# Odd layer attention: the rest of the queries on both partition halves, second score product over 128 rows

## The chip, the cores and the metric

The kernel runs on one core of one Trainium2 chip, as one program for the whole computation. The metric is the device time of one execution in microseconds (us), taken as the median of the runs shown; less is better. TensorE (PE in the profile) does the matrix products and the transposes, VectorE (DVE) and ScalarE (ACT) read its results out of PSUM, GpSimd (POOL) works on SBUF only, and SyncE (SP) issues the DMAs. Each engine works off its own queue in the order in which the program put it there.

## What is computed

Two blocks of layers on 512 tokens of width 1024. The first block has four layers, the second has an even and an odd one, each followed by a feed-forward part. The change lies in the mixer of the odd layer, which has eight heads of neighbourhood attention and eight heads of grouped-query attention, each with 64 features. Cut to what matters:

```python
def odd_mixer(u_lat, u_ctx, need_ctx, w_in, w_out, rpb, q_norm, k_norm, rope):
    lat = split_cols(u_lat @ w_in, ODD_SPLITS)
    ctx = split_cols(u_ctx @ w_in, ODD_SPLITS)
    c_lat = neighbourhood_attention(q, k, v, k_ctx, v_ctx, rpb)      # 8 heads: bias, 512 keys + 256 context keys
    d_lat = blocked_attention(qd_l, concat(kd_c, kd_l), concat(vd_c, vd_l), GQA_DIM ** -0.5)   # 8 heads, 2 key heads
    return concat(c_lat, d_lat) @ w_out

# per head, for 128 queries at a time
s = (q @ k.T) * scale (+ bias)      # 768 keys: 512 tokens and 256 of the context
p = softmax(s)
o = p @ v
```

## The kernel before

Products are taken in the type float32r. To keep the precision of float32, an operand x is held as two parts, the leading part h (x rounded to float32r) and the rest l = x - h, and a product is the sum of the products of the parts.

The odd layer has the stages `oddkv` (keys and values), `oddq` (queries), `odda` (attention), `out` (output projection) and then `ffn`. In `odda` (`odd_attn`, `odd_pair`, `attend`) the 16 heads are taken in 8 pairs, pairs 0 to 3 neighbourhood heads, pairs 4 to 7 grouped-query heads. The two heads e = 0, 1 of a pair lie on partitions 0 to 63 and 64 to 127. Each pair goes through 4 query tiles of 128 queries. For a query tile and a head, `attend` has two score products, one of 512 and one of 256 keys, each in a PSUM bank of its own; then `softmax` (DVE takes the maximum, line 852, or with the bias added, line 1071; then the negated maximum, line 857; ACT the exponential with its sum, line 864; DVE the reciprocal, lines 869 and 871); then `turned` (TensorE transposes the result, line 889; DVE copies 256 columns out, line 891, ACT 512, line 893); then the product with the values (line 1080). At the end of a pair, line 878 spreads the reciprocals over the partitions, line 1085 copies them and line 1086 multiplies. Four PSUM banks (`pp`) serve the scores, four (`pa`) all else.

The operands of a pair are made by `odd_operands` one pair ahead. `attn_keys` gives, for head e, one tile with the leading part of its keys on the head's own half of the partitions and the rest of its keys on the other half (lines 1871, 1872, both on DVE). `attn_queries` gives, for head e, a tile `hi[e]` with the leading part of its queries on both halves (line 1856 on DVE, line 1857 on ACT), and one tile `lo` for both heads, the rest of head e's queries on its own half (line 1858 on POOL). So one product over 128 rows, line 1881, yields qh·kh + qh·kl, and a second one over the head's own 64 rows, line 1882, adds ql·kh. Both add up in the same PSUM bank:

```python
nc.tensor.matmul(ps, qh[e][:, s], kap, start=True, stop=False)      # 128 rows, line 1881
nc.tensor.matmul(ps, ql[r, s], kap[r], start=False, stop=True)      # 64 rows, line 1882
```

The operand tiles are taken from the pools that also hold weights, by tag, with `NBUF` buffers each: `cwr` 3, `cwh` 2, `cwl` 2, `wh` 4, `wl` 4. Pairs with an even number use the tags with a c, odd ones the others (the keys of the grouped-query heads are made once for two pairs). A new tile of a tag waits until the tile whose buffer it takes has been read for the last time. The order of the instructions on each engine is laid down when the program is built, by a planner that puts them in the order of its own estimate of the times.

Of the kernel before, what the change touches and what calls it, by code (L numbers as in the profile page):

```python
# [22 lines left out]
SEQ = 512  # L23
# [12 lines left out]
class Split:  # L36
    """An operand held as two float32r parts, [128, k, n] in pieces along k."""
# [11 lines left out]
class Residual:  # L49
    """The residual stream: in SBUF between a layer's end and the next norm, else in DRAM."""  # L50
# [13 lines left out]
    def store(self, t, dst=None):  # L64
        """Token tile t goes to DRAM (a new version at t = 0)."""
        if t == 0:
            n = self.core.nm("res_" + self.key)
            self.new = dst if dst is not None else self.core.dp.tile([self.nt * 128, D], F32, name=n, tag=n)
        n = 1 if dst is None else 2
        for i in range(n):  # L70
            cs = slice(i * D // n, (i + 1) * D // n)
            self.core.nc.sync.dma_start(self.new[t * 128:(t + 1) * 128, cs], self(t)[:, cs])
        if t == self.nt - 1:
            self.src = self.new


class Core:
# [21 lines left out]
    def phase(self, name, gen):  # L99
        """gen, its tiles named after it."""  # L100
# [21 lines left out]
    def bank(self, use, shape, dt):  # L122
        """A PSUM bank of the groups that the use has, by turns."""
# [15 lines left out]
    def setup(self):  # L139
        """What the first norm waits for: its condition, its modulation, x."""  # L140
# [27 lines left out]
        for v in (1, 0):  # L168
# [5 lines left out]
            # column 2g + h of the vector lies in row 32g of half h  # L174
# [10 lines left out]
    def setup2(self):  # L185
# [9 lines left out]
        # a norm's root is taken of the sum of squares, not of their mean  # L195
# [6 lines left out]
    def condition(self, name, srcs):  # L202
        """silu of condition columns, padded to 32 columns so that a column group is whole."""
# [12 lines left out]
    def columns(self, key, parts):  # L216
        """Vectors of 128-blocks -> columns over partitions, one transpose for all."""
# [17 lines left out]
    def rstd1(self, ss, n, eps=EPS):  # L235
        """(ss / n + eps) ** -0.5 for a [128, 1] column."""
# [7 lines left out]
    def rstdN(self, ss, n, width, c=1.0, eps=EPS):  # L244
        """c * (ss / n + eps) ** -0.5 for [128, width]."""
# [13 lines left out]
    def lo_engine(self, ph):  # L259
        """The engine of the next subtraction, by turns."""  # L260
        ph = self.sk + ph
        pat = LO.get(ph, LO.get(self.sk, LO[""]))
        i = self.nlo[ph] = self.nlo.get(ph, -1) + 1
        return self.nc.gpsimd if pat[i % len(pat)] == "p" else self.nc.vector

    def weights(self, W, k0, nk, c0, n, held=False):
        """Rows k0*128.. of W, columns c0.., as split parts [128, nk, n]."""
# [7 lines left out]
    def wsplit(self, src, nk, n, held=False):  # L275
        """src [128, a, b] in DRAM, a * b = nk * n -> split parts [128, nk, n]. Held ones leave the next ones room."""
# [11 lines left out]
    def proj_tok(self, H, nt, W, K, c0, n, out, r0=0, each=None, inturn=False, lead=1):  # L288
        """out[0] = PSUM tiles [128, 2, n], two token tiles each, by columns c0..c0+n (rows r0*128.. of W).
        With each, out[0] is by token tiles and each(t) is called for every one; in turn, one is finished  # L290
        before the next starts."""
# [32 lines left out]
        for i in range(0, len(ks), lead):  # L324
            ws = [(k0, nk, self.weights(W, r0 + k0, nk, c0, n)) for k0, nk in ks[i:i + lead]]
            for t in range(nt):
                # a PSUM bank holds two token tiles as one accumulation group
# [7 lines left out]
    def proj_T(self, H, ntok, W, K, cols, out, m=128):  # L335
        """out[0] = PSUM [m, ntok] each, columns cols[i].. of W on partitions."""
# [5 lines left out]
    def cols_T(self, o, H, W, K, c0, m):  # L342
        """o = columns c0..c0+m of H @ W, transposed."""
# [12 lines left out]
    def halves_T(self, o, H, Ws, K, n):  # L356
        """cols_T of the first 128 columns of several matrices, one half of the tokens before the other."""
# [15 lines left out]
    def mods(self, scr, cname, W, ncond, v):  # L373
        """Vector v of cond @ W into DRAM scr [ncond, .. * 1024] (bias not yet added)."""
# [20 lines left out]
    # Background work: queues of generators, of which step takes a step now and then.  # L395
# [20 lines left out]
    def drain(self, gen):  # L416
        """Runs gen, background work after each of its steps."""
# [7 lines left out]
    def mod_cols(self, scr, ic, b, v0, pre):  # L425
        """Columns A = pre * (1 + scale), B = shift; shift at vector v0, scale at v0 + 1."""
# [13 lines left out]
    def gate_row(self, scr, ic, b, v, post):  # L440
        """32 * gate * post over all partitions, [128, 1024]."""
# [21 lines left out]
    def prenorm(self, x, nt, m):  # L463
        """x(t) [128, 1024] per token tile -> H, a Split of the modulated norm, transposed.
        Returns (H, step), step(t) for each token tile once x(t) is there."""
# [17 lines left out]
        def turn(xs, s):  # L483
            """Token tiles xs, normed, into H."""
# [26 lines left out]
    def normed(self, x):  # L511
        """x / its root of the sum of squares."""
# [14 lines left out]
    def rstd2(self, a, b):  # L527
        """(a + b) ** -0.5 for columns."""
# [6 lines left out]
    def outproj(self, O, nt, W, K, x, gg, nxt=None, dst=None):  # L535
        """x(t) += rms(O @ W) * gg; nxt() gives the norm that follows, fed tile by tile. Returns its H."""
# [30 lines left out]
    def first(self, n):  # L567
        """What is put out now comes before the last n instructions."""
        return self.tc.high_priority(offset=n) if n else nullcontext()

    def partial(self, ssp, nt):
        """The first three parts of the sums of squares, and what keeps the root from zero."""
# [6 lines left out]
    def postnorm(self, yg, a, b, x):  # L579
        """x += (a + b) ** -0.5 * yg."""  # L580
# [6 lines left out]
    def silu2(self, dst, z):  # L587
        """dst = 2 * silu(z), z may sit in PSUM."""
# [4 lines left out]
    def newO(self, nt=4):  # L593
        """A mixer's output, transposed, in pieces that come into being with their first write."""
# [3 lines left out]
    def Opiece(self, O, k, nt=4):  # L598
        """Where rows k * 128.. of the output go."""
# [12 lines left out]
    def Odone(self, O, p, nt=4):  # L612
        """Piece p is complete: split."""
# [7 lines left out]
    def gla(self, H, j, O):  # L621
# [13 lines left out]
        for h in range(4):  # L635
            v = []
            if h == 0:
                # a projection by token tiles is the first to start
# [21 lines left out]
    def gla_decay(self, H, j, b):  # L660
        """b: per head the logarithm of the decay, summed up in chunks of 128, times 16."""
        nc, A = self.nc, self.A
        W = A["gla_w_in"][j]
        # low-rank decay
# [31 lines left out]
    def gla_pairs(self, b, qT, kT, out):  # L696
# [9 lines left out]
        for lv in range(7):  # L706
# [14 lines left out]
            for c in range(4):  # L721
                # the later tokens of a pair of blocks against the earlier ones
# [120 lines left out]
    def softmax(self, heads, scale, rl, first=None):  # L843
        """heads: (P, parts) each, P [128, ..] taking exp(scale * (s - max)) of the parts in turn;
        rl [128, heads] takes 1 / sum. first: per head a [128, 2] whose column 0 is the first part's maximum."""
# [27 lines left out]
    def rows(self, rl):  # L873
        """Columns rl [128, query tile, 2] of two heads as rows over the heads' partitions, in PSUM."""
# [7 lines left out]
    def turned(self, pt, P, n):  # L882
        """pt [128, n] = P', by 128 columns."""
# [12 lines left out]
    def fox_forget(self, H):  # L896
        """-8 times the summed logarithms of the forget gates, [head, token] in DRAM."""
# [22 lines left out]
    def fox(self, H, O):  # L920
        nc, A = self.nc, self.A
        W = A["fox_w_in"][0]
        # the gains of queries and keys, over two heads
# [7 lines left out]
        for g in range(4):  # L931
# [16 lines left out]
            # a projection that needs no norm follows each that does  # L948
# [24 lines left out]
    def fox_queries(self, x, gain):  # L973
        """A head pair's queries x [128, token tile, 128] as parts, transposed, [.., head, token]: h and l; h and
        two ones. The gain is that of queries and keys."""
# [11 lines left out]
    def fox_decays(self, F):  # L987
        """A tile for fox_keys' second result, with the parts of the heads' F."""
# [8 lines left out]
    def fox_keys(self, x, KB):  # L997
        """Keys, likewise: h and h; l and the parts of the heads' F."""
# [10 lines left out]
    def fox_pair(self, hp, ops, v, zg, out):  # L1009
        """Attention of heads 2hp and 2hp + 1 of a group; zg: twice their gates, transposed."""  # L1010
# [4 lines left out]
        for it in range(4):  # L1015
# [4 lines left out]
            for e in range(2):  # L1020
                ps = (self.psP if FOXS else self.psA)()
                # at least 256 columns, where float32r takes a cycle each
# [19 lines left out]
    def transposes(self, src, nt):  # L1042
        """src(t) [128, m] per token tile -> PSUM [m, nt * 128]."""
# [7 lines left out]
    def attend(self, out, nq, scores, keys, v, nj, scale, bias=None):  # L1051
        """scores(e, it, ps, keys): query tile it's products; keys(e) -> [(AP, n)], one PSUM bank each; v(e, j) [128, 64].
        out [128, nq * 128]: the heads' outputs on partition halves."""
# [35 lines left out]
    def rope(self, x, n, cs):  # L1089
        """In place on x [128, t, h, 2n], cs = (cos, sin) [128, t, n]."""  # L1090
# [11 lines left out]
    def gsplit(self, hi, lo, src, g):  # L1102
        """Split src * g, g per partition."""
# [63 lines left out]
    def gdn_proj(self, H, nt, key, st):  # L1167
        """Projections, convolution, normalisation: q, k, v by tokens, decays by rows and columns."""
# [28 lines left out]
        # suffix sums for the backward rows: total - prefix + own  # L1197
# [23 lines left out]
        # what the later stages of a head pair or group take waits in DRAM for its turn  # L1221
# [23 lines left out]
    def gdn_cols(self, H, st, cols):  # L1245
        """q, k or v (0, 1, 2) of head pairs: [(which, pair)]. A projection's convolution runs under the next
        one's products, and only then it is turned."""
# [25 lines left out]
    def gdn_put(self, st, sv, cols):  # L1273
        """Column blocks by tokens, normalised, to DRAM."""
# [31 lines left out]
    # The delta rule runs in chunks, both directions, on groups of nh heads (nh * nt = 8). A unit u of  # L1306
    # a group is a head and a token tile; with a half e of the tile's partitions it is a chunk of 64
    # tokens. Direction d = 1 runs from the last token to the first.
# [4 lines left out]
    def gdn_decay(self, st, g):  # L1313
        """exp(-|gc_p - gc_f|) between the tokens of a group's chunks."""
# [21 lines left out]
    def gdn_front(self, st, g, E):  # L1336
        """Decayed products k k' and k q' of a group's chunks, the former cut in 32 x 32 blocks."""
# [43 lines left out]
    def gdn_subst(self, st, s):  # L1381
        """(I + M)^-1 of the 32 x 32 diagonal blocks of two groups, one block a partition, by forward
        substitution; a backward block is taken transposed. M[c, s] = beta_c Gd[c, s];
        R = (I + M)^-1 diag(beta)."""
# [38 lines left out]
    def gdn_steps(self, st, g, out):  # L1423
        """The inverse's blocks put together, the step matrices."""
# [855 lines left out]
```

## Time and profile before

| | us |
|---|---|
| median of 3 runs | 3319.11 |
| lowest and highest of the 3 | 3316.0, 3320.16 |
| span of the profiled execution, first to last instruction | 3315.4 |
| PE busy in the span | 3154.1 (95%) |
| PE weight load busy | 2704.3 (82%) |
| DVE busy | 1699.2 (51%) |
| ACT busy | 1451.7 (44%) |
| POOL busy | 1307.3 (39%) |

The profiled execution's span is 3315.4 us; what its time holds beside the span is not shown by itself. In the profile, a line such as `L1882` is a line of the kernel, `odda.pp` a tile of stage `odda`, `64*128` the rows and columns of the array that a product takes, and the figures behind it partitions x elements of what is streamed. The matmul records overlap, since their ends are modelled: the time that a product takes from the next one is read from the starts, or from the chain, whose pieces follow each other without overlap. The chain (or critical chain) is the work that ended last, followed back: each piece is what the next one waited for.

### The profile page before, as it was taken

The numbers are of one execution on the slowest core, as the hardware profiler recorded it, in microseconds if no ns is written. First come the engines' busy times: TensorE is split into PE (matmuls) and PEld (weight loads), VectorE is DVE, ScalarE is ACT, GpSimd is POOL, SyncE is SP. The second block draws the span as 40 slices with busy tenths as digits, with TensorE's granted clock in tenths as the row PEclk, the third lists the DMA queues.
The fourth block names the chain that finished last, engine by engine and source line by source line (L and its number), as shares of the span: only waits on it lengthen the run. The fifth ranks groups of instructions, "written<-read, shape, count | busy, mean of one in ns | idle before, by whom it ended". The sixth has DMA issues, their size and how long they took to land.

```text
span 3315.4 us, 63038 instructions
## 1 busy us (share of the span) xinstructions
PE 3154.1 (95%) x24399; PEld 2704.3 (82%) x24399; DVE 1699.2 (51%) x3578; ACT 1451.7 (44%) x3189; POOL 1307.3 (39%) x1320
## 2 busy tenths in 40 slices
PE   7999999899999999988989999899999989999999
PEld 4878889778778778887877899889889956789898
DVE  3744564454555555657888667531215476541112
ACT  3434544455444533345545544543325246543323
POOL 2544453322222344443642123554446510154445
PEclk9999999999999999998999999899999979999999
DMA  7355645754436524444753344433333310043332
GB/s 239 87 159 185 194 144 164 234 173 125 147 111 198 162 81 132 153 117 126 188 172 110 86 131 114 155 115 94 117 101 124 102 39 1 25 142 94 98 119 89
DMA packets 487155, 426.36 MB, mean 129 GB/s; under 512 B 108038, under 2 KB 441065, under 8 KB 486857
## 3 DMA queue, kind: packets, MB, share of 16 engines
q1 hardware_dynamic: 486857, 422.35, 42.5%
q8 instruction: 192, 3.15, 0.4%
q14 instruction: 106, 0.87, 0.1%
HBM read 383.66 MB, written 38.03 MB: 127 GB/s over the span
## 4 chain that ended last, share of the span: by engine, by line
PE 75%; DVE 11%; DMA 5%; ACT 4%; issue 3%; POOL 2%; SPq 1%; POOLq 0%; DVEq 0%; ACTq 0%
PE ffn.pp L352 6%; PE ffn.pp L351 6%; PE ffn.pp L353 5%; PE ffn.pp L308 3%; PE ffn.pp L307 3%; PE ffn.pp L309 3%; PE mods.pa L386 3%; PE out.pp L307 2%; PE out.pp L309 2%; PE out.pp L308 2%; DMA mods.wm<-in_w_mod_dram 2%; PE odda.pa L889 1%; PE fox.pp L308 1%; PE fox.pp L309 1%; PE fox.pp L307 1%
## 5 line engine op out<-in xcount | busy, mean ns | idle before, releaser
L257 POOL TENSOR_TENSOR ffn.wl<-ffn.wr,ffn.wh 128x512 fp32r<-128x512 f32 x258 | 333.5, 1294 | 355.0 <-ACT ffn.wh L256 355.0
L256 ACT ACTIVATE ffn.wh<-ffn.wr 128x512 fp32r<-128x512 f32 x258 | 162.5, 631 | 354.9 <-PE ffn.pp L353 144.3
L351 PE MATMUL ffn.pp<-pre.t,ffn.wh 128*128 128x512 f32 x672 | 261.5, 389 | 0.0
L352 PE MATMUL ffn.pp<-pre.t,ffn.wl 128*128 128x512 f32 x672 | 261.5, 389 | 0.0
L353 PE MATMUL ffn.pp<-pre.t,ffn.wh 128*128 128x512 f32 x672 | 261.4, 389 | 0.0
L308 PE MATMUL ffn.pp<-ffn.wl,ffn.t 128*128 128x256 f32 x656 | 185.3, 283 | 0.0
L309 PE MATMUL ffn.pp<-ffn.wh,ffn.t 128*128 128x256 f32 x656 | 184.9, 283 | 0.0
L307 PE MATMUL ffn.pp<-ffn.wh,ffn.t 128*128 128x256 f32 x656 | 184.7, 283 | 0.0
L591 DVE SCALAR_TENSOR_TENSOR ffn.t<-ffn.t,ffn.pp 128x512 f32<-128x512 f32 (+1 forms) x66 | 39.4, 596 | 252.2 <-ACT ffn.t L590 252.1
L257 POOL TENSOR_TENSOR gla.wl<-gla.wr,gla.wh 128x512 fp32r<-128x512 f32 x66 | 87.2, 1321 | 163.7 <-ACT gla.wh L256 158.5
L307 PE MATMUL gla.pp<-gla.wh,pre.t 128*128 128x256 f32 x512 | 149.4, 292 | 0.7 <-ACT gla.t L644 0.4
L308 PE MATMUL gla.pp<-gla.wl,pre.t 128*128 128x256 f32 x512 | 148.8, 291 | 0.0
L309 PE MATMUL gla.pp<-gla.wh,pre.t 128*128 128x256 f32 x512 | 148.4, 291 | 0.0
L353 PEld LDWEIGHTS ffn.pp<-pre.t,ffn.wh 128*128 128x128 f32 x672 | 126.2, 188 | 26.2
L351 PEld LDWEIGHTS ffn.pp<-pre.t,ffn.wh 128*128 128x128 f32 x672 | 126.2, 188 | 26.1
L352 PEld LDWEIGHTS ffn.pp<-pre.t,ffn.wl 128*128 128x128 f32 x672 | 126.2, 188 | 25.8
L257 POOL TENSOR_TENSOR ffn.cwl<-ffn.cwr,ffn.cwh 128x512 fp32r<-128x512 f32 x44 | 60.3, 1370 | 212.4 <-ACT ffn.cwh L256 183.9
L386 PE MATMUL mods.pa<-mods.wm,cond_c 128*32 128x256 f32 x1408 | 121.4, 398 | 16.8 <-DMA mods.wm<-in_w_mod_dram 16.7
L1133 DVE SCALAR_TENSOR_TENSOR ffn.t<-ffn.t,ffn.pp 128x512 f32<-128x512 f32 (+1 forms) x66 | 39.4, 597 | 176.3 <-PE ffn.pp L353 175.7
L256 ACT ACTIVATE ffn.cwh<-ffn.cwr 128x512 fp32r<-128x512 f32 x132 | 82.9, 632 | 102.8 <-PE ffn.pp L353 43.0
L308 PEld LDWEIGHTS ffn.pp<-ffn.wl,ffn.t 128*128 128x128 f32 x656 | 125.9, 192 | 0.2
L307 PEld LDWEIGHTS ffn.pp<-ffn.wh,ffn.t 128*128 128x128 f32 x656 | 125.6, 192 | 0.2
(786 smaller groups left out, 10843.8 us busy)
## 6 DMA issues: line engine op xcount, KB each, us to landing
mods.wm<-in_w_mod_dram SPq DMA_DIRECT2D x176, 512.0 KB
gla.wr<-in_gla_w_in_dram SPq DMA_DIRECT2D x96, 256.0 KB
ffn.wr<-in_w_ffn_gate_dram SPq DMA_DIRECT2D x88, 256.0 KB
ffn.wr<-in_w_ffn_up_dram SPq DMA_DIRECT2D x88, 256.0 KB
ffn.wr<-in_w_ffn_down_dram SPq DMA_DIRECT2D x88, 256.0 KB
fox.wr<-in_fox_w_in_dram SPq DMA_DIRECT2D x64, 256.0 KB
sgu.wr<-in_sgu_w_in_dram SPq DMA_DIRECT2D x48, 256.0 KB
out.res_x<-out.t SPq DMA_DIRECT2D x24, 512.0 KB
```

What stands on the lines that cost most here:

```text
L256: nc.scalar.activation(hi, src, AF.Copy)
L257: (lo_eng or nc.vector).tensor_tensor(lo, src, hi.bitcast(F32), op=ALU.subtract)
L307: nc.tensor.matmul(o, H.hi(kk, s), w[0][:, k], start=(kk == 0 and first), stop=False)
L308: nc.tensor.matmul(o, H.hi(kk, s), w[1][:, k], start=False, stop=False)
L309: nc.tensor.matmul(o, H.lo(kk, s), w[0][:, k], start=False, stop=(kk == K - 1 and last))
L351: nc.tensor.matmul(o, wh[:, k], H.hi(kk), start=(kk == 0), stop=False)
L352: nc.tensor.matmul(o, wl[:, k], H.hi(kk), start=False, stop=False)
L353: nc.tensor.matmul(o, wh[:, k], H.lo(kk), start=False, stop=(kk == K - 1))
L386: nc.tensor.matmul(ps[g * 32:(g + 1) * 32, :256], pad[:, j, :], ws[j][:, g * 256:(g + 1) * 256], start=(j == 0), stop=(j == 7))
L591: nc.vector.scalar_tensor_tensor(dst, dst, 1.0, z, ALU.add, ALU.mult)
L889: nc.tensor.transpose(pz[:, j:j + 128], P[:, j0 + j:j0 + j + 128], self.ident)
L1133: nc.vector.scalar_tensor_tensor(f, sg, 0.5, o[1], ALU.mult, ALU.mult)
```

## The change

`attn_queries` holds the rest of the queries in one tile for each head. The subtraction of line 1858 writes it on the head's own half as before, and a new instruction on ACT copies it to the other half. Line 1882 then takes all 128 rows of that tile and of the keys, and so adds ql·kh + ql·kl. The tags of the rests are `cwr` and `cwh` in even pairs (before, `cwh`), `wh` and `wl` in odd ones (before, `wh`). The diff also takes out comments and docstrings all over the file and leaves the line numbers up to this place; of code it has only this:

```diff
@@ def attn_queries(self, q, par):
         hi = [self.w(("cwr", "wh")[par], 1, n)[:, 0] for _ in range(2)]
-        lo = self.w(("cwh", "wh")[par], 1, n)[:, 0]
+        lo = [self.w(tag, 1, n)[:, 0] for tag in (("cwr", "cwh"), ("wh", "wl"))[par]]
         for e in range(2):
             r, z = self.H4(e), self.H4(1 - e)
             nc.vector.tensor_copy(hi[e][r], q[r])
             nc.scalar.copy(hi[e][z], q[r])
-            nc.gpsimd.tensor_tensor(lo[r], q[r], hi[e][r].bitcast(F32), op=ALU.subtract)
+            nc.gpsimd.tensor_tensor(lo[e][r], q[r], hi[e][r].bitcast(F32), op=ALU.subtract)
+            nc.scalar.copy(lo[e][z], lo[e][r].bitcast(F32))
         return hi, lo
@@ def odd_pair(self, hp, st, O, q, keys):
         def scores(e, it, ps, kap):
-            s, r = slice(it * 128, (it + 1) * 128), self.H4(e)
+            s = slice(it * 128, (it + 1) * 128)
+
             nc.tensor.matmul(ps, qh[e][:, s], kap, start=True, stop=False)
-            nc.tensor.matmul(ps, ql[r, s], kap[r], start=False, stop=True)
+            nc.tensor.matmul(ps, ql[e][:, s], kap, start=False, stop=True)
```

## Rows read from the trace of the kernel before

**Rows 1.** The page: the span, and the shares of the whole chain by engine

```profile
span 3315.4 us, 63038 instructions
...
PE 75%; DVE 11%; DMA 5%; ACT 4%; issue 3%; POOL 2%; SPq 1%; POOLq 0%; DVEq 0%; ACTq 0%
```

**Rows 2.** Stretches: length, busy us of PE, PEld, DVE, ACT, POOL, clock, DMA

```profile
2663.40:2683.40 20.00, 20.00 (x71) 12.37 (x72) 10.54 (x37) 7.11 (x21) 0.00 (x0) 0.58 0.10 30
...
2700.80:2719.90 19.10, 19.10 (x87) 12.67 (x88) 9.86 (x36) 9.28 (x27) 0.00 (x0) 0.65 0.00 0
2719.90:2727.40 7.50, 7.32 (x57) 5.08 (x57) 7.15 (x19) 3.93 (x10) 2.66 (x2) 1.00 0.01 2
...
2801.80:2824.60 22.80, 22.65 (x165) 15.41 (x165) 13.58 (x46) 14.16 (x40) 0.88 (x1) 1.00 0.01 2
...
2663.40:2882.20 218.80, 212.35 (x1512) 145.33 (x1513) 144.03 (x466) 126.81 (x344) 25.56 (x17) 0.93 0.03 9
```

**Rows 3.** The chain between 2700 and 2880 us, shares by line

```profile
by line: PE odda.pa L889 23.4%; PE odda.pa L1080 18.6%; PE odda.pp L1882 18.5%; PE odda.pp L1881 12.5%; DVE odda.mx L852 3.7%; issue 3.5%; PE odda.pa L878 2.8%; ACT odda.at L864 2.3%; DVE odda.at L891 2.2%; DVE odda.wh L1871 1.7%; DVE odda.
```

**Rows 4.** The chain in order of time, pair 5: start us, us, what

```profile
2815.19 0.59 PE odda.pa L889 x4
2815.77 0.23 PE odda.pp L1881
2816.00 0.42 PE odda.pp L1882
2816.42 0.37 PE odda.pa L889 x2
2816.79 0.12 PE odda.pp L1881
2816.91 0.31 PE odda.pp L1882
...
2818.46 0.31 PE odda.pp L1881
...
2821.50 0.58 PE odda.pa L1080 x6
2822.09 0.43 PE odda.pp L1882
```

**Rows 5.** Source line 1882, one of its forms: duration ns least/median/most, starts, form

```profile
L1882 PE MATMUL odda.pp<-odda.wl,odda.wh x24: 490/497/792, 2689.2 to 2875.4; 64*128 64x512 f32 x24
```

**Rows 6.** Source line 1025, the second score product of stage fox

```profile
L1025 PE MATMUL fox.pp<-fox.t,fox.t x64: 278/342/628, 728.3 to 1011.7; 66*128 66x256 f32 x32, 66*128 66x384 f32 x16, 66*128 66x512 f32 x16
```

**Rows 7.** The chain at the end of stage fox, first products of out

```profile
1011.63 0.23 PE fox.pp L1024
1011.86 0.23 PE fox.pp L1025
...
1013.35 0.12 PE out.pp L308
```

**Rows 8.** Timeline of DVE in pair 5

```profile
2818.50 0.69 DVE L852 TENSOR_REDUCE odda.mx<-odda.pp 128x1 f32<-128x512 f32 x1 [0.62 <-PE odda.pp L1882]
...
2824.59 1.05 DVE L852 TENSOR_REDUCE odda.mx<-odda.pp 128x1 f32<-128x512 f32 x2 [0.21 <-PE odda.pp L1882]
```

**Rows 9.** The chain at the start of pair 0

```profile
2664.49 0.72 PE odda.pp L1881
...
2670.90 0.43 PE odda.pp L1881
```

**Rows 10.** Source lines 1857 and 1858, and the waits between 2688 and 2877

```profile
L1857 ACT CAST odda.wh<-oddq.t x8: 616/617/618, 2658.7 to 2825.3; 64x512 fp32r<-64x512 f32 x8
...
L1858 POOL TENSOR_TENSOR odda.wh<-oddq.t,odda.wh x8: 1262/1278/1377, 2659.0 to 2826.6; 64x512 fp32r<-64x512 f32 x8
...
POOL odda.wh L1858 <- PE odda.pp L1881: 78.0, 3, 30.4
```

**Rows 11.** The stretch ahead of the second half-clock one, columns of rows 2

```profile
2695.00:2700.00 5.00, 3.54 (x46) 2.79 (x44) 2.29 (x8) 1.24 (x4) 0.00 (x0) 1.00 0.00 0
```

## The prediction

> **What bounds the kernel now.** I read the page first: the chain that ended last is TensorE for 75% of a span of 3315.4 us, and DVE follows with 11% [rows 1]. The average says nothing of the stage that is changed, so next come the stretches of the attention, from the first score product at 2663.4 us to the last product with the values near 2882.2 us. In these 218.8 us PE shows 212.4 us busy, DVE 144.0, ACT 126.8, POOL 25.6, and DMA is at rest [rows 2]. The chain inside it, by line, is again TensorE: transposes (889) 23.4%, products with the values (1080) 18.6%, the score products 18.5% (1882) and 12.5% (1881) [rows 3]. What the reader is to notice is that line 1882, with half the rows, takes more of the chain than line 1881, which streams the same columns.
>
> The chain in order of time tells why [rows 4]. A 512-column product of line 1881 that follows a transpose costs the chain 0.23 us; the product of line 1882 behind it, as wide, 0.42. A pair of transposes behind line 1882 takes 0.37, though a group of four takes 0.59, so that two more cost 0.22 and some 0.17 to 0.19 us are paid once for coming from line 1882. With 256 columns it is 0.12 for line 1881 behind a transpose, 0.31 for line 1882, and 0.31 for line 1881 behind line 1882. So each passage into line 1882 costs about 0.19 us, and each passage out of it as much, whatever the width. Line 1882 takes 64 rows of the array [rows 5]; what stands around it takes 128.
>
> Is it the rows, or the second product of a sum as such? Stage fox answers: its second score product adds into the bank of the first too, has 66 rows [rows 6], and costs 0.23 us behind a first one of 0.23; the out stage's products of 256 columns follow each other at 0.12 [rows 7]. Products of full array rows, with new weights each, follow without the 0.19. The page TensorEngine Tiling (Array Packing) of the Trainium skill, under Key Properties, says that changing the tiling mode drains TensorE, and this trace agrees with 0.19 us a change.
>
> **The change part by part.**
>
> *Line 1882 over 128 rows.* No instruction is added on TensorE, no column more is streamed. Passages between 128 rows and 64 rows vanish; passages to and from lines 1080 and 878 stay, since these take 64 columns of the array. Take two query tiles of pair 5 as the pattern. From 2815.19 to 2819.45 us the chain is TensorE throughout: 0.59, 0.23, 0.42, 0.37, 0.12, 0.31, then the same for the other head's first product, then 0.31, 0.31, 0.37 [rows 4], 4.26 us. With all rows at 128 this is 0.40 + 0.23 + 0.23 + 0.20 + 0.12 + 0.12 + 0.40 + 0.23 + 0.23 + 0.12 + 0.12 + 0.20 = 2.6; keeping 0.17 for the passage to line 1080 after it, 2.8: 1.46 us less. In the next tile six products of line 1080 stand between 1881 and 1882 [rows 4], so that the first passage stays, and I get 0.74 less up to the last maximum. Raw: 2.2 us in two tiles, and there are 16 such couples (8 pairs of 4 tiles): 35 us.
>
> *What is late next.* In the first tile DVE begins the maximum of the second head after 0.62 us of idling on line 1882, in the second tile after 0.21 [rows 8]; that idle time is the room it has. Behind the first head's scores it has a maximum of 0.69, a copy, a maximum, a sum, the second head's maximum of 0.69 and the negated maximum: about 2.6 us in a row, by the same timeline. Followed with these durations, the exponential of the next tile comes 0.47 us earlier, its transposes about 1.1 (they had waited on line 1080, and now wait on the exponential), and the second tile adds only its 0.21. So 1.3 of the 2.2 us come through; DVE takes the rest. For pairs 4 to 7, 8 couples: 10.4 us. In pairs 0 to 3 DVE also splits keys, and stretches such as 2719.9 to 2727.4 belong to it, 7.15 of 7.50 us busy [rows 2]; I give nothing there. Some 36 us of their chain are TensorE at full clock: at 1.3 in 13, 3.6 us.
>
> *The half-clock stretches.* From 2663.4 to about 2680 and from 2701 to 2714 us the granted clock is 0.5 (means 0.58 and 0.65 over the stretches) [rows 2], the 1.2 GHz level. There a 512-column product costs 0.43 behind a transpose and 0.72 behind line 1882 [rows 9], so a passage costs 0.29. The chain there is all TensorE; its pieces in order of time show 16 such passages in the first stretch and 8 in the second: 4.6 and 2.3 us, with the full-clock ends of both stretches 5.6 and 4.0. DVE is busy for half of each, so nearly all comes through: I take 5 and 3. If the clock comes back at the same moment rather than after the same work, a passage there is worth 0.19 and the two give 2.4 us less.
>
> *The new copies on ACT.* Sixteen copies of 64x512, one for each head. The nearest row is line 1857, a copy of that shape between halves: 0.617 us [rows 10]; 9.9 us in all, on an engine that is busy 126.8 of 218.8. Each waits for POOL's subtraction, 1.28 us, which itself waits for the buffers of the pair before (78.0 us in three waits) [rows 10]. Behind the copy in ACT's queue stand exponentials, and for those DVE's sums and TensorE's transposes wait. Bounds: nothing, where ACT idles, up to 0.62 + 1.28 us for each copy that is queued just ahead of an exponential, 30 us for all. The scores themselves have a pair of time before they need the result, as the operands are made a pair ahead; only pairs 0 and 1 do not, and there DVE's keys come last, at 2663.4. I take 1 us, near the low end, since POOL's waits end where ACT has gaps.
>
> *Buffers.* A third `cwr` and a third `wl` tile are held. Even pairs used to have one `cwr` to spare, so a part of their operands could be made earlier; the pair of lead remains, cost taken as nothing. If that cover is gone, one subtraction, cast and copy (2.5 us) shows once in a pair of that kind. At the end `wl` keeps one buffer less free for the out stage's first weights, but their leading parts wait for `wh` until the end of the scores anyway.
>
> **Sum.** 10.4 + 3.6 + 5 + 3 - 1 = 21 us off 3315.4, so a span near 3294. The median of the runs lies 3.7 us above that span; 3319.1 - 21 = **3298 us**.
>
> **Rivals.**
>
> *All of it comes through* (chance 0.12): DVE and ACT find an order that hides them, since 144.0 and 126.8 us of work fit into 180 us. 35 us and 2.4 for the half clock: 3282; if the stretch of 13 us from 2701 falls away too, 6.5 more: 3275. For it: the planner may lay the order anew. Against: rows 8.
>
> *DVE and ACT give all back at full clock* (0.12): only the half-clock stretches pay, 8 us: 3311. For it: DVE's share in stretches between pairs; against: 22.65 of 22.80 us PE and 13.58 DVE in pairs 4 and 5 [rows 2].
>
> *The load of the weights is not hidden after all* (0.04). If what costs 0.19 is that the weights of line 1882 meet rows of the array that the running product still uses, all 128 rows would still meet them, no passage becomes cheaper, and the copies are left: 3320. Against it stand 0.23 behind 0.23 in fox and 0.12 in out [rows 7]. The page TensorE: Matmul & The Clock Gate, Part 3, The mechanism, has such a rule: weight loads overlap running products only where the row groups differ. It would give this rival; the trace contradicts it with the 0.23.
>
> *The clock falls* (0.06, slower). With TensorE done sooner, it waits more in small pieces. The half clock from 2701 us came after a stretch in which PE was busy 3.54 of 5 us [rows 11]. Some 160 us of TensorE work remain; each us of it at half clock costs half a us. It decides once more than 42 us beyond today's 30 run at half clock: then the 21 are gone; with 65 it is 3331. Against it: the same columns in less time make TensorE denser, not sparser.
>
> **How the numbers follow.** The forecast has 0.66, with 3286 to 3307 for itself. The range reaches to the first two rivals, and takes in the 2.4 us of the clock and some of ACT's 30: 3276 to 3312. About 6.6 us (0.2%) is what a measurement of this kernel can tell from no change. Faster by more: 0.66 + 0.12 + half of 0.12 = 0.84. Same: 0.06 + 0.04 = 0.10. Slower: 0.06.
>
> **What would show it.** Right: line 1882 at 0.23 and 0.12 in the chain behind 1881, transposes behind it at 0.10 each, PE's busy share between 2663 us and the end of the stage down to about 85%, DVE's share of the chain up, the stage near 198 us, all else as before. Wrong: 0.42 and 0.31 still there (no passage saved); copies of `lo` in the chain, or exponentials waiting behind them for POOL; a granted clock of 0.5 in more of the stage; stages before 2640 us that take another time, which would mean that the planner moved more than this.

## The result, and the profile after

The changed kernel takes **3281.99 us** in the median (3276.99 to 3285.36) where the kernel before takes 3319.06: a ratio of 0.9893 with a 95% interval of 0.9873 to 0.9914, 28 to 42 us less. The profiled execution took 3278.63 us, with a span of 3276.8 (before: 3315.4 [rows 1]). In the changed kernel the score products are lines 1883 and 1884, the key operands 1872 and 1873, and the new copy is line 1859.

The page of the changed kernel, span and shares of the chain:

```profile
span 3276.8 us, 63046 instructions
...
PE 74%; DVE 11%; DMA 5%; ACT 4%; issue 3%; POOL 2%; SPq 1%; DVEq 0%; POOLq 0%; ACTq 0%
```

Averages over the whole span hardly move. So I take one measure of the stage for all kernels: from the last product of the queries to the last multiplication of line 1086, the end of pair 7. Before it runs from 2652.0 to 2887.9, 235.9 us; after from 2653.9 to 2849.8, **195.9 us, 40.0 less**. What follows takes 427.5 us before and 427.0 after. The part ahead ends between 2644.5 and 2661.6 us in the traces below though its work is the same, so medians carry some us that are not the stage's; the same kernel in two traces gave 195.9 and 197.5.

Stretches (columns of rows 2): first the kernel before, from where the score products begin to follow each other (2663.4 us, as in [rows 2]) to the end of pair 7; then the changed kernel, the same and the stage:

```profile
2663.40:2888.60 225.20, 218.75 (x1580) 151.09 (x1581) 145.86 (x469) 128.62 (x348) 25.56 (x17) 0.93 0.03 10
```

```profile
2665.10:2850.50 185.40, 170.50 (x1581) 138.87 (x1582) 145.42 (x474) 135.86 (x360) 25.94 (x17) 0.99 0.04 12
2653.90:2849.80 195.90, 171.85 (x1586) 139.38 (x1585) 153.57 (x486) 143.53 (x374) 31.49 (x21) 0.97 0.10 24
```

The last row of [rows 2] ends at 2882.2 us, some 5 us short of the last products with the values, so the row above stands in its place. PE is busy 170.5 us where it was 218.8, with the same number of matmuls of `odda`; DVE does what it did, in less time; ACT has the 16 copies more, 135.9 us for 128.6; and the mean granted clock is 0.99 where it was 0.93.

The chain through two query tiles of pair 5, the same two as [rows 4], in the changed kernel:

```profile
2787.59 0.58 PE odda.pa L889 x4
2788.18 0.23 PE odda.pp L1883
2788.41 0.23 PE odda.pp L1884
2788.65 0.22 PE odda.pa L889 x2
2788.87 0.12 PE odda.pp L1883
2788.99 0.12 PE odda.pp L1884
...
2790.48 1.78 PE odda.pa L1080 x24
2792.26 0.59 PE odda.pa L889 x4
...
2798.44 0.66 PE odda.pa L889 x4
```

The second product is down from 0.42 to 0.23 us and from 0.31 to 0.12, two transposes behind it from 0.37 to 0.22. The two tiles take 10.85 us (2787.59 to 2798.44); before they took 12.98 (2815.19 to 2828.17).

All kernels side by side. "Half clock" is PE's busy time that ran at the 1.2 GHz level in the one profiled execution of each kernel, worked out from 1-us stretches between 2640 and 2880 us (busy time times 2·(1 − granted clock), summed). At the 2.4 GHz level it would have taken half as long. Each ratio is to the kernel before as timed beside that kernel (medians of 3319.1 to 3320.0 us).

| kernel | median us | ratio to before (95%) | stage us | half clock us |
|---|---|---|---|---|
| before | 3319.06 | | 235.9 | 31.6 |
| after | 3281.99 | 0.9893 (0.9873 to 0.9914) | 195.9 | 4.0 |
| e11_after_again | 3280.60 | 0.9888 (0.9864 to 0.9911) | 197.5 | 7.3 |
| e1_copies_alone | 3314.82 | 0.9990 (0.9975 to 1.0004) | 233.1 | 28.7 |
| e2_late_pairs | 3299.62 | 0.9941 (0.9921 to 0.9961) | 223.8 | 41.9 |
| e3_early_pairs | 3292.10 | 0.9912 (0.9888 to 0.9937) | 213.3 | 9.9 |
| e9_passages_back | 3334.69 | 1.0043 (1.0026 to 1.0060) | 252.9 | 47.9 |
| e4_no_second | 3271.20 | 0.9854 (0.9835 to 0.9873) | 192.9 | 11.9 |
| e12_no_second_again | 3276.70 | 0.9871 (0.9845 to 0.9898) | 193.0 | 15.0 |
| e5_pool_half | 3305.94 | 0.9946 (0.9925 to 0.9966) | 218.9 | 25.8 |
| e6_warm_after | 3284.11 | 0.9881 (0.9860 to 0.9901) | 200.8 | 10.0 |
| e7_warm_64 | 3319.63 | 1.0001 (0.9985 to 1.0018) | 236.6 | 34.0 |
| e8_keys_act | 3284.86 | 0.9886 (0.9862 to 0.9910) | 198.6 | 13.2 |

### The profile page after: what moved, and what is told of

Read it like the earlier page. It is cut to its first block, busy times and chain, and to the rows that moved or that the text cites. A ratio compares the mean times of both kernels' runs of the same rounds, so it can differ in the third digit from the quotient of the medians.

```text
span 3276.8 us, 63046 instructions
## 1 busy us (share of the span) xinstructions
PE 3100.1 (95%) x24399; PEld 2687.7 (82%) x24399; DVE 1691.3 (52%) x3578; ACT 1460.2 (45%) x3205; POOL 1308.6 (40%) x1320
## 4 chain that ended last, share of the span: by engine, by line
PE 74%; DVE 11%; DMA 5%; ACT 4%; issue 3%; POOL 2%; SPq 1%; DVEq 0%; POOLq 0%; ACTq 0%
PE ffn.pp L352 6%; PE ffn.pp L351 6%; PE ffn.pp L353 6%; PE ffn.pp L308 3%; PE ffn.pp L307 3%; PE ffn.pp L309 3%; PE mods.pa L386 3%; PE out.pp L307 2%; PE out.pp L309 2%; PE out.pp L308 2%; DMA mods.wm<-in_w_mod_dram 2%; PE fox.pp L308 1%; PE fox.pp L309 1%; PE fox.pp L307 1%; PE sgu.pp L307 1%
## 5 line engine op out<-in xcount | busy, mean ns | idle before, releaser
L257 POOL TENSOR_TENSOR gla.wl<-gla.wr,gla.wh 128x512 fp32r<-128x512 f32 x66 | 87.0, 1319 | 163.2 <-ACT gla.wh L256 153.6
```

Source lines behind the costliest of these rows:

```text
L257: (lo_eng or nc.vector).tensor_tensor(lo, src, hi.bitcast(F32), op=ALU.subtract)
```

## The experiments

The measured 37 us stand against a forecast of 21. The theories: (a) the passages between 128 and 64 rows are the cause, at the price that the rows of before show; (b) rather the copies, the buffers or the new order that the planner makes of them; (c) the clock, which the forecast had taken as given. All edits are made to the changed kernel.

### Copies and buffers, without the 128 rows (e1)

```diff
-            nc.tensor.matmul(ps, ql[e][:, s], kap, start=False, stop=True)
+            nc.tensor.matmul(ps, ql[e][self.H4(e), s], kap[self.H4(e)], start=False, stop=True)
```

> The changed kernel with its tiles and its copies on ACT, but the second score product over the head's own 64 rows, as before the change (the copied halves are not read). Theory A: the gain is the passages between 64 and 128 rows alone. Then nothing of it is left: 3316 to 3325 us, 0 to 6 us beyond the kernel before for the copies, and in the chain 0.42 and 0.31 us for the second product. Rival B: the order that the planner lays with the new copies and buffers (the operands of pair 1 made at another place) gave part of it: then the time stays under 3305 us. Clock: if it comes back early because the products follow each other without passages, this kernel shows the half clock for some 17 us after the first scores, as the kernel before did; if the order does it, the clock is back within 5 us of the first dense products, as in the changed kernel.

Measured: 3314.8 us, a ratio of 0.9990 whose interval holds 1; stage 233.1 against 235.9. So the copies cost nothing that shows, and order and buffers alone bring at most those 2.8 us of the stage. Nearly the whole gain needs the 128 rows.

### Half of the pairs each (e2, e3)

```diff
+            r = self.H4(e) if hp < 4 else slice(None)      # e2; in e3: if hp >= 4
-            nc.tensor.matmul(ps, ql[e][:, s], kap, start=False, stop=True)
+            nc.tensor.matmul(ps, ql[e][r, s], kap[r], start=False, stop=True)
```

> The second product over 128 rows in pairs 4 to 7 only, over 64 rows in pairs 0 to 3. By the prediction's step (1.3 of 2.2 us in two query tiles come through, 8 couples) it lies 10 us under the kernel with the copies alone. By the starts of the pairs in the trace of the changed kernel, where 6.9, 4.8, 4.5 and 2.4 us went in pairs 4 to 7, it lies 18 us under it; then DVE takes nothing back there.

> The second product over 128 rows in pairs 0 to 3 only. By the prediction's steps (5 and 3 us in the half-clock stretches, 3.6 elsewhere) it lies 12 us under the kernel with the copies alone; by the trace of the changed kernel 21 us, of which some 8 to 10 come from half-clock stretches that are no longer there, and then its granted clock shows 0.5 for less than 6 us after the first scores.

Measured against e1: e2 is 15.2 us faster in the median, e3 22.7. The times of pairs 4 to 7 alone, from the end of pair 3 to the end of pair 7, are told apart cleanly, since in these pairs all instructions stand in one order on every engine in e1, e2, e3 and after, and the clock is full there: 99.2 us with 64 rows (e1 and e3), 85.15 and 85.2 with 128 (e2 and after). That is **14.1 us less, 1.76 for each couple of tiles**, where the prediction gave 1.3.

In the early pairs e3 gains more than passages alone can give. Its stage is 19.8 us shorter than that of e1, and its half clock falls from 28.7 to 9.9 us, which is worth half of the difference, 9.4. The other 10.4 are left for the passages, together with the planner's order, which in pairs 0 to 3 is not the same in e1 and e3; the prediction had 11.6 for them (3.6 + 5 + 3). In the stage, e2 gains only 9.3 us, though its late pairs gain 14.1: in its profiled execution a third stretch of half clock, 2750 to 2761, stands in the early pairs, which still have 64 rows. These pairs are the same in e1 and e2, order included, so 28.7 and 41.9 us of half clock also show how far two executions of the same work can lie apart.

### The passages put back, with 128 rows kept (e9)

```diff
             nc.tensor.matmul(ps, qh[e][:, s], kap, start=True, stop=False)
+            z = self.H4(1 - e)
+            nc.tensor.matmul(ps[:, :16], ql[e][z, s], kap[z, :16], start=False, stop=False)
             nc.tensor.matmul(ps, ql[e][:, s], kap, start=False, stop=True)
```

> The changed kernel with one more small product between the two of each score: 16 columns over the 64 rows of the other half, which adds the product of the two rests once more for 16 keys. Both large products keep 128 rows; only the passages between 128 and 64 rows are back, 256 of them. If passages are the cause, not the rows of the large product, the gain goes: 128 times two passages of 0.19 us is 49 us of TensorE, 3315 to 3335 us, and the half clock is back for more than 10 us after the first scores and again later. If only the small products' own length counts (some 0.06 us each), 8 us: 3290.

Measured: 3334.7 us, the gain is gone and 15.6 us more. The chain in pair 5 of e9 (line 1885 is the 16-column product over 64 rows, 1886 the second product over 128):

```profile
2802.39 0.23 PE odda.pp L1883
2802.62 0.20 PE odda.pp L1885
2802.82 0.43 PE odda.pp L1886
2803.25 0.22 PE odda.pa L889 x2
2803.47 0.12 PE odda.pp L1883
2803.59 0.20 PE odda.pp L1885
2803.79 0.32 PE odda.pp L1886
```

A product of 16 columns costs 0.20 us, and the full one behind it, 0.23 and 0.12 in the changed kernel, costs 0.43 and 0.32 again: 0.20 more for either width. The price belongs to the change of rows, not to the half-filled product or its columns. The evidence is these pieces, not the total: the planner lays another order here, in the late pairs too. The page TensorEngine Tiling (Array Packing) of the Trainium skill, Key Properties, has the drain at a change of mode; here it measures 0.20 us.

### The second product left out (e4, e12), and the changed kernel once more (e11)

```diff
-            nc.tensor.matmul(ps, qh[e][:, s], kap, start=True, stop=False)
-            nc.tensor.matmul(ps, ql[e][:, s], kap, start=False, stop=True)
+            nc.tensor.matmul(ps, qh[e][:, s], kap, start=True, stop=True)
```

> The changed kernel without the second score product at all: the rest of the queries is left out of the scores (it is still made and copied). 64 products of 0.23 us and 64 of 0.12 us are gone, 22 us of TensorE. If TensorE is still what is late next in the attention, 15 to 22 us less than the changed kernel: 3260 to 3267 us. If DVE and ACT have become what is late next, as the prediction held, less than 10 us: 3272 us or more.

> The changed kernel once more, to stand beside the other two on the same chip: 3277 to 3285 us; half clock for less than 6 us of work, since two traces with 128 rows in the early pairs (this kernel and the one with early pairs only) showed 4 to 10 us, and three with 64 rows 29 to 42.

> The changed kernel without the second score product once more, beside the changed kernel: from the end of the queries' products to the end of the attention the two traces differed by 3 us only, the medians by 11. If the stage is what counts, 3 to 6 us under the changed kernel on the same chip; 22 us less of TensorE would then be hidden by DVE and ACT to three quarters or more.

The changed kernel once more takes 3280.6 us, as expected, with 7.3 us at half clock where less than 6 was. In e4 and e12, with 0.23 + 0.12 us for each of 64 pairs of products, some 22 us of TensorE work are gone. The stage is 3.0 us shorter (e4 against after) and 4.5 (e12 against e11); the medians say 10.8 and 3.9 less. Of the lost gain the clock takes a part: e4 and e12 have 8 us more at half clock than their partners, worth 4. The rest is in the chain. First e4's stage (columns of rows 2), then its chain between 2655 and 2843 us by line, then the same of the changed kernel, 2655 to 2850:

```profile
2649.40:2842.30 192.90, 158.11 (x1458) 123.39 (x1458) 153.12 (x487) 141.73 (x374) 30.94 (x21) 0.95 0.09 25
```

```profile
by line: DVE odda.mx L852 15.1%; PE odda.pa L1080 11.2%; PE odda.pa L889 10.9%; ACT odda.at L864 8.8%; DVE odda.at L891 6.3%; issue 5.6%; PE odda.pp L1883 4.9%; DVE odda.t L1071 4.7%; DVE odda.ls L869 3.1%; DVE odda.wh L1872 2.9%; DVE odda.
```

```profile
by line: PE odda.pa L1080 18.5%; PE odda.pa L889 17.1%; PE odda.pp L1883 8.6%; PE odda.pp L1884 7.8%; DVE odda.mx L852 5.5%; issue 4.7%; ACT odda.at L864 4.3%; PE odda.pa L878 3.6%; DVE odda.t L1071 3.4%; DVE odda.at L891 3.1%; DVE odda.wh 
```

In the changed kernel TensorE still leads, and the second product has gone from 18.5% (between 2700 and 2880 us, [rows 3]) to 7.8%; in e4 the maximum on DVE leads and ACT's exponential has doubled its share. So DVE and ACT, which the prediction named, are late next; in the changed kernel itself they are so only in places.

### The second half made by POOL (e5), the keys' casts given to ACT (e8)

```diff
-            nc.scalar.copy(lo[e][z], lo[e][r].bitcast(F32))                                       # e5
+            nc.gpsimd.tensor_tensor(lo[e][z], q[r], hi[e][r].bitcast(F32), op=ALU.subtract)
-KHI = lambda nc: nc.vector.tensor_copy                                                            # e8
+KHI = lambda nc: nc.scalar.copy
```

> The changed kernel, but the second half of the rests is made on POOL, by a second subtraction of 1.28 us from the same inputs, in place of the copy on ACT: 9.9 us less on ACT, 20 us more on POOL, which is idle for most of the stage. If the copies on ACT cost nothing, as the kernel with the copies alone says, within 5 us of the changed kernel. If they stand in the way of exponentials, 5 to 10 us less. If POOL's work slows what DVE does beside it (casts of 0.42 us took up to 1.4 in the trace of before while POOL was busy), some us more.

> The changed kernel with the leading part of the keys (line 1872) made on ACT in place of DVE: 24 casts of 0.42 to 1.3 us off DVE, some 13 us, and as many copies of 0.4 to 0.6 us on ACT. If DVE is what is late next in pairs 0 to 3, as the prediction held, 4 to 10 us less than the changed kernel; if ACT and DVE bound it alike, within 3 us; if ACT's exponentials wait behind the casts, more.

e5 loses 24 us of the gain, stage 218.9. ACT's 16 copies are gone, but POOL does twice its work, and DVE slows beside it: 165.9 us busy in the stage, 153.6 in the changed kernel. The 25.8 us at half clock, worth 10.9 more than those of the changed kernel, are about half of the loss. Two casts of the first keys, in the changed kernel and in e5 (duration ns least/median/most, starts, form), and what stands on POOL and DVE at that time in e5:

```profile
L1872 DVE CAST oddq.cwh<-.t x2: 286/288/291, 2662.2 to 2662.5; 64x256 fp32r<-64x256 f32 x2
```

```profile
L1872 DVE CAST oddq.cwh<-.t x2: 1282/1288/1293, 2666.3 to 2667.6; 64x256 fp32r<-64x256 f32 x2
```

```profile
2666.19 1.26 POOL L1858 TENSOR_TENSOR oddq.cwh<-oddq.t,oddq.cwr 64x512 fp32r<-64x512 f32 x1
2667.51 1.26 POOL L1859 TENSOR_TENSOR oddq.cwh<-oddq.t,oddq.cwr 64x512 fp32r<-64x512 f32 x1
```

```profile
2666.32 2.61 DVE L1872 CAST oddq.cwh<-.t 64x256 fp32r<-64x256 f32 x2
```

Each cast lasts as long as the subtraction on POOL beside which it stands, not 0.29 us. So where the copy runs matters: with it on ACT, POOL is done when these two casts come, and they keep their 0.29. (Two others, from 2659.6 us on, stand beside POOL in the changed kernel too, and take 2.52 us together.) ACT waits for POOL's result only in these (idle us, times, ahead of line 1859):

```profile
  POOL odda.cwh L1858: 3.1, 2
  POOL odda.wh L1858: 0.5, 1
```

e8 moves the 24 key casts from DVE to ACT: 3284.9 us, stage 2.7 us longer than after; nothing is gained. DVE has 154 and ACT 144 us busy of 196, so the move relieves one and burdens the other. But e8 also has 9.2 us more at half clock, worth 4.6, so that the move may bring some 2 us; these runs cannot tell that from nothing.

### TensorE kept busy ahead of the attention (e6, e7)

```diff
+        d, H = self.psA(), st["H"]          # e6: in the changed kernel; e7: in e1. H is the input of the queries
+        for i in range(40):
+            nc.tensor.matmul(d, H.hi(0, slice(0, 128)), H.hi(0), start=True, stop=True)
```

> The changed kernel with 40 products of 512 columns that nothing reads put on TensorE between the last transposes of the queries and the first scores, where TensorE waits for DVE some 9 us. They keep its clock up. The half clock of the changed kernel covers only 3.4 us of work after the first scores: 1 to 3 us less, 3279 to 3281, if the products are done before the first keys are there; some us more if they are not.

> The same 40 products in the kernel with the copies alone (second product over 64 rows). There the half clock covered 15 us of work after the first scores and 9 more later. If the half clock is a price of the cold start only, these go: 7 to 12 us less than that kernel, 3303 to 3308, and the gain of the early pairs (22.7 us) is to a third or a half the clock's. If passages let the clock fall by themselves, 0.5 is back within the stage though it started at 1.0, and the time stays above 3310.

In e1 and in the changed kernel TensorE waits while the first keys are made, and the clock stands at half at the first scores. e7 keeps it at the upper level up to there with products that nobody reads. Stretches of e7 (columns of rows 2):

```profile
2664.00:2674.00 10.00, 9.43 (x38) 6.60 (x36) 9.59 (x15) 4.81 (x9) 4.40 (x4) 1.00 0.92 216
2674.00:2682.00 8.00, 7.80 (x21) 4.69 (x22) 5.01 (x21) 3.72 (x11) 0.00 (x0) 0.57 0.07 25
2758.00:2763.00 5.00, 3.21 (x42) 2.41 (x40) 2.60 (x8) 1.40 (x4) 0.00 (x0) 1.00 0.00 0
2763.00:2777.00 14.00, 13.95 (x57) 10.06 (x57) 6.00 (x24) 5.69 (x17) 0.00 (x0) 0.51 0.00 1
```

The clock falls all the same, at 2674 from full speed, and again at 2705 and 2763: 34 us at half clock, 3319.6 us in the median. With 128 rows (e6) the same products buy nothing: 3284.1, stage 4.9 longer than after. So it is not the idle time at the start alone that keeps the clock low in the kernels with 64 rows.

## Why the prediction was right or wrong

**That the passages are the cost, and their price: right.** 0.42 and 0.31 became 0.23 and 0.12 as written, e1 without the 128 rows stands at the time of before, and e9 with the passages put back loses everything. The rival of the weight load falls by the same 0.23 and 0.12.

**The time: 3298 forecast, 3282 measured, inside the range.** The range held it because it had been drawn as far as the rivals; the sum itself was 16 us off. The time came out where the rival "all of it comes through" stood (3282, or 3275), by part of that rival's reasons. Two terms of the sum were too small, and the larger of them had been taken as nothing:

| term | forecast | measured |
|---|---|---|
| passages in pairs 4 to 7 | 10.4 | 14.1 (e1 to e2, e3 to after) |
| passages in pairs 0 to 3 (3.6 + 5 + 3) | 11.6 | 10.4 (e1 to e3, clock taken off) |
| less work at half clock | 0 | 13.8 (half of 31.6 − 4.0) |
| copies, order, buffers | −1 | +1.3 (before to e1: 2.8 in the stage, of which 1.5 are clock), the median unclear |

The four measured terms make 39.6, against 40.0 for the whole stage. The first is good to some tenths of a us; the clock's, and with it the second and the last, rest on one execution of each kernel, and e1 and e2 alone lie 13 us of half clock apart, worth 6.6.

**The half-clock stretches: the step that failed.** The prediction took their length as given and asked only what a passage costs in them; that they might be a result of the passages it held as a footnote, for one stretch, in a rival. The stretches, first of e1 and then of the changed kernel, show it:

```profile
2665.00:2675.00 10.00, 10.00 (x25) 5.82 (x25) 5.65 (x21) 5.59 (x17) 0.00 (x0) 0.50 0.00 0
2675.00:2685.00 10.00, 10.00 (x67) 7.16 (x67) 5.72 (x18) 4.66 (x13) 1.27 (x1) 0.81 0.01 2
2695.00:2705.00 10.00, 8.16 (x38) 5.05 (x34) 6.37 (x22) 4.54 (x13) 0.00 (x0) 0.71 0.01 2
2705.00:2715.00 10.00, 10.00 (x65) 6.99 (x64) 4.67 (x18) 4.73 (x16) 0.00 (x0) 0.78 0.00 0
```

```profile
2665.00:2675.00 10.00, 9.24 (x61) 7.28 (x62) 9.05 (x33) 5.88 (x19) 0.00 (x0) 0.82 0.19 55
2675.00:2685.00 10.00, 10.00 (x87) 7.69 (x87) 9.68 (x29) 7.63 (x19) 2.81 (x2) 1.00 0.01 2
2695.00:2705.00 10.00, 10.00 (x89) 7.76 (x88) 8.54 (x32) 8.18 (x22) 1.28 (x1) 1.00 0.00 0
2705.00:2715.00 10.00, 8.69 (x92) 6.87 (x91) 9.33 (x27) 6.74 (x16) 1.27 (x1) 1.00 0.01 2
```

Both begin at half clock, after TensorE has waited for the first operands. In e1 PE shows 10.00 us of work in 10, at 0.50, and the clock is back only near 2679; in the changed kernel it is back near 2669, and the second fall, which e1 has at 2699 to 2710, does not come. The split goes through all kernels: with passages in the early pairs (before, e1, e2, e7, e9) 29 to 48 us run at half clock; without (after, e3, e4, e6, e8, e11, e12) 4 to 15. Outside stands e5, with no passages and 26 us, where TensorE waits more (PE busy 183 of 219 us). That the half clock goes with the passages is shown from both sides, by e1 to e3 (28.7 to 9.9) and by after to e9 (4.0 to 47.9); the two groups do not overlap, though each kernel has one profiled execution. The planner's order changes with them, in the early pairs from e1 to e3 and throughout from after to e9, so its part is not shown, and by what means passages hold the clock down stays open. The rival "the clock falls" named the right thing to watch, with the wrong sign.

**What is late next: right for the couple it was read from, too small as a pattern for all eight.** For the couple of pair 5 the forecast was 2.2 us raw and 1.3 of it let through. Against the kernel before, 2.13 came (12.98 to 10.85). But 0.82 of that is there without the 128 rows: e1 has the order of the changed kernel in these pairs, with all 24 products of line 1080 in the couple's first tile where the kernel before has 18 and 6, and its couple takes 12.16. From e1 to the changed kernel only the rows differ, and they give 1.31. The four query tiles of pair 5, first in e1, then in the changed kernel (columns of rows 2; the couple is the second and third):

```profile
2805.70:2812.63 6.93, 6.78 (x51) 4.56 (x52) 4.31 (x13) 3.43 (x10) 0.00 (x0) 1.00 0.00 1
2812.63:2818.36 5.73, 5.73 (x45) 3.92 (x46) 3.30 (x12) 3.37 (x11) 0.00 (x0) 1.00 0.00 0
2818.36:2824.79 6.43, 5.96 (x45) 4.04 (x45) 4.14 (x13) 4.59 (x12) 2.53 (x2) 1.00 0.01 3
2824.79:2831.25 6.46, 6.46 (x55) 4.64 (x56) 3.72 (x14) 5.38 (x17) 0.00 (x0) 1.00 0.00 0
```

```profile
2781.91:2787.59 5.68, 5.53 (x51) 4.38 (x52) 3.78 (x12) 3.47 (x11) 0.00 (x0) 1.00 0.00 0
2787.59:2792.26 4.67, 4.67 (x46) 3.97 (x46) 3.32 (x13) 3.62 (x13) 0.00 (x0) 1.00 0.01 2
2792.26:2798.44 6.18, 4.74 (x44) 3.89 (x45) 4.51 (x14) 4.83 (x12) 2.53 (x2) 1.00 0.01 3
2798.44:2803.48 5.04, 5.04 (x55) 4.49 (x56) 3.65 (x14) 4.73 (x14) 0.00 (x0) 1.00 0.00 0
```

The couple's tiles give 1.06 and 0.25 us; the prediction had the transposes of the second 1.1 us earlier, and 0.21 for that tile. The other two tiles, which it did not follow, give 1.25 and 1.42. TensorE is busy nearly throughout in three of the four tiles; only in the third, where POOL and DVE also make operands of the next pair, does it wait, 1.44 us of 6.18, while DVE works in a row to the negated maximum and ACT then takes the exponential. DVE's timeline in that tile of the changed kernel:

```profile
2795.09 0.67 DVE L852 TENSOR_REDUCE odda.mx<-odda.pp 128x1 f32<-128x512 f32 x1
2795.78 0.70 DVE L1856 CAST odda.wh<-oddq.t 64x512 fp32r<-64x512 f32 x1
2796.51 0.43 DVE L852 TENSOR_REDUCE odda.mx<-odda.pp 128x1 f32<-128x256 f32 x1
2796.85 0.41 DVE L891 COPY odda.at<-odda.pa 128x256 f32<-128x256 f32 x1
2797.30 0.33 DVE L857 TENSOR_SCALAR odda.nm<-odda.mx 128x1 f32<-128x1 f32 x2
```

So the limit that was forecast is real, but in pair 5 it binds in one tile of four, and the couple with that tile was taken as the pattern for all eight: 1.3 for each, where 1.76 came in the mean. A smaller error lies in the "2.6 us in a row": it adds the lengths of DVE's records, but records that follow each other overlap, the last copy above starting 0.34 us behind a maximum of 0.43. The same row in the changed kernel takes 2.2 us, from the start of the first maximum at 2788.69 to the end of the negated maximum at 2790.89.

**Copies and buffers: right that they cost little,** and too careful with 1 us: e1 shows no loss. Of what was to show a failure, copies in the chain and exponentials behind POOL, only the 3.6 us of ACT's waits above are found. PE's share was to fall to 85% from the first score on; it is 92% (170.5 of 185.4), since the stretch shrank with it. The "198" for the stage was 21 off the 218.8 of [rows 2], which ends too early; to the end of pair 7 it would have been 21 off 225.2, 204, and 185 came.

**No better version was found.** Only the kernels that leave the second product out are faster than the changed one. Untried is an order of TensorE in which the products with the values cover DVE's row in the tile that makes the next pair's operands.

## What to carry to other kernels

Price a TensorE instruction by the chain, behind each kind of neighbour: a product over fewer array rows than its neighbours can cost more than one over all rows that carries idle or added rows, and doubling an operand on an engine with room pays for it. When an edit takes stalls out of TensorE near a stretch of low clock, forecast two cases, the stretch as it is and the stretch gone, with a chance for each. When asking what is late next, follow the whole period (here the four tiles of a pair), not the one piece that shows the limit, and sum an engine's work from starts, not from record lengths. When a control run keeps the order but not the change, compare with it and not with the kernel before: here 0.8 of the 2.1 us that one couple seemed to gain came without the change, with the planner's new order.

## What the runs showed of the hardware

The granted clock can stay at the 1.2 GHz level while PE shows no idle time: 10.00 us busy of 10 at 0.50 in e1, with 25 matmuls. It fell from the full level in e7 at 2763, behind a stretch with 3.21 us busy of 5; then it stayed there for 14 us with 13.95 of them busy. In the kernels without passages in the early pairs such stretches make 4 to 15 us, but for the 26 of e5.

A cast on DVE of 64x256 took 288 ns alone and 1288 ns beside a subtraction on POOL of 1.26 us. The page SBUF — State Buffer of the Trainium skill, Who interferes with whom, says that DVE and GpSimd share a pair of ports which one instruction holds to its end; this trace agrees, each of the two casts ending some 0.15 us behind POOL's instruction.
